# Stick-breaking heads with queries on the partitions: a running sum on VectorE in place of triangular products, and shorter reciprocal roots

## The chip, the cores and the metric

The kernel runs on one core of one Trainium2 chip. The metric is the device time of one execution in microseconds, as the median of three runs. TensorE (PE in the profile) multiplies matrices into PSUM, VectorE (DVE) does elementwise work, ScalarE (ACT) activation functions and casts, SyncE (SP) issues the DMAs.

## The reference

Two layers, each of four additions to a residual of 512 tokens by 1024 channels: a gated feed-forward network, a mixer, a cross attention to 256 memory rows, a second feed-forward network. The change lies in the mixer, which runs 8 stick-breaking heads of width 64 and 4 gated delta-rule heads of width 128 beside each other:

```python
z = einsum('bhtd,bhsd->bhts', qb, kb) * scale
causal = s_idx < t_idx
log_beta = log_sigmoid(z)
log_1m_beta = where(causal, log_beta - z, 0.0)
between = cumsum(log_1m_beta, axis=3, reverse=True) - log_1m_beta
a = where(causal, exp(log_beta + between), 0.0)
out = einsum('bhts,bhsd->bhtd', a, vb)
```

So the weight of key s for query t is exp(z minus the sum of softplus(z) over all keys from s to t). The delta-rule heads (GDN below) normalise q and k, solve a triangular system within a chunk of 128 tokens, and carry a state over four chunks; the outputs of both kinds are normalised by reciprocal roots and go into one output projection.

## The kernel before

Activations are held transposed, channels on the partitions, 512 tokens along the free axis. Every dense weight is split into a rounded part and a rest (`unit`: ScalarE casts, `split_low` L169 subtracts on VectorE), and each dense product is three TensorE products of 512 columns (`mm3`). All TensorE products go through `mm` (L118), transposes through `transpose` (L496).

The order of TensorE's instructions is written out by the program itself: `weave` runs four generators (the norm, `mixer_gdn`, `mixer_sb`, `mixer_dense`) on a planned clock `clk`, which `mm` advances by a planned cost. A generator that yields a number of nanoseconds is taken up again when the clock has passed it, one that yields names waits for `mark`s; the first ready one in that order emits its instructions, so dense projections fill what the chains leave. The numbers set the order alone; on the chip each instruction waits for semaphores. VectorE, ScalarE and the DMA queue are ordered by the framework's scheduler.

`sb_pair` (L583) handles two heads of 64. Scores lie with keys on the partitions: `scores` puts key blocks into three PSUM banks (`SBB`: widths 256, 384+128, 512 queries), each block being a mask product and two products with a split operand. ScalarE makes softplus by Abs (L621), Exp (L622) and Ln (L623), VectorE adds the positive part (L624) and the result is split again. `sums` (L635) then subtracts the running sum over keys on TensorE: each block gets products of `ntri` or `nones` with both parts of every later block, 20 products a head. `weights` takes Exp (L642) and splits; `values` (L649) multiplies by V with `mm3`, 12 products a head, V standing in `vpad` between zeros so that both heads add into one bank.

`gdn_head` (L728) is the chain of one GDN head: norms, a blockwise triangular solve (L809 to L850), four chunk steps (L864 to L886). Its small roots, and those of `sb_pair`, come from `rsqrt`, whose `newton` (L218) is 11 small VectorE operations, each needing the one before.

`mixer_dense` (L948) emits the projections of heads 0 to 3 in turn; from head 2 on it waits for `q0`, `q1` (a GDN head's last chunk) and `qk0`, `qk1` (a pair's last scores). The output projection (`project_out`, L449) takes the pairs' results as `sb0` to `sb3` come, and only its first two output blocks run ahead of `sb3`.

Of the kernel before, what the change touches and what calls it, by code (L numbers as in the profile page):

```python
# [52 lines left out]
class Trunk:  # L53
# [67 lines left out]
    def setup(self):  # L121
# [23 lines left out]
        self.cr = self.sb([P, 2, P], "cr", F32R)  # L145
        self.cb = self.sb([P, 3, P], "cb", BF16)
        self.ntri, self.nones = (self.cr[:, i, :] for i in range(2))
        self.nsb, self.ngd, self.idb = (self.cb[:, i, :] for i in range(3))
        nc.gpsimd.tensor_copy(self.ntri, stage[:, 0:P])
        nc.gpsimd.tensor_scalar(out=self.nones, in0=self.ones, scalar1=-1.0, scalar2=None, op0=ALU.mult)  # L150
# [347 lines left out]
    def gates(self, layer):  # L498
# [36 lines left out]
        yield 12800.0  # L535
# [45 lines left out]
    SBB = (((2, 0, 256),), ((1, 0, 384), (3, 384, 128)), ((0, 0, 512),))  # L581

    def sb_pair(self, layer, pair):  # L583
        nc = self.nc
        mm = self.mm
        t1s = ("s15", "s16", "s17")
        names = [f"s{i}" for i in range(19, 27)]
# [4 lines left out]
        hi, lo = (t.rearrange("p t (j d) -> p t j d", j=3)[:, :, 0:3:2, :] for t in self.vpad)  # L592
        self.split_act(hi, src)
        self.split_low(lo, src, hi)
        self.mark(f"vt{pair}")
        kk, qq, ql = self.qk[pair]
        zs, sp, aa = {}, {}, {}
        av = None

        def split(t, w):  # L600
# [5 lines left out]
            self.split_act(hi, t)  # L606
            self.split_low(lo, t, hi)
            return hi, lo

        def scores(j, n):  # L610
            bl = self.SBB[n]
            z = zs[j, n] = self.bank("at", self.AT)
            w = sum(b[2] for b in bl)
            for i, (s, c, width) in enumerate(bl):
                mm(z[:, c:c + P], self.idb, self.nsb, start=i == 0, stop=False, skip_group_check=True)
                ks = slice(s * P, (s + 1) * P)
                mm(z[:, c:c + width], kk[j][:, ks], qq[j][:, s * P:], start=False, stop=False, skip_group_check=True)
                mm(z[:, c:c + width], kk[j][:, ks], ql[j][:, s * P:], start=False, stop=True, skip_group_check=True)
                yield 200.0
            t1 = self.slot(self.turn("t1", t1s))[:, :w]  # L620
            nc.scalar.activation(t1, z[:, :w], AF.Abs)  # L621
            nc.scalar.activation(t1, t1, AF.Exp, scale=-1.0)  # L622
            nc.scalar.activation(t1, t1, AF.Ln, bias=1.0)  # L623
            nc.vector.scalar_tensor_tensor(out=t1, in0=z[:, :w], scalar=0.0, in1=t1,  # L624
                                           op0=ALU.max, op1=ALU.add)
            hi, lo = split(t1, w)
            for s, c, width in bl:
                sp[j, s] = (hi[:, c:c + width], lo[:, c:c + width])

        def sums(j, n):  # L630
            bl, z = self.SBB[n], zs[j, n]
            for s, c, width in bl:
                for s2 in range(s, NT):
                    for part in sp[j, s2]:
                        mm(z[:, c + (s2 - s) * P:c + width], self.ntri if s2 == s else self.nones, part,  # L635
                           start=False, stop=True, skip_group_check=True)
                    yield 0

        def weights(j, n):
            w = sum(b[2] for b in self.SBB[n])  # L640
            a = self.slot(self.turn("t1", t1s))[:, :w]
            nc.scalar.activation(a, zs[j, n][:, :w], AF.Exp)  # L642
            aa[j, n] = split(a, w)

        def values(j, n):
            hi, lo = aa[j, n]
            for i, (s, c, width) in enumerate(self.SBB[n]):
                vs = slice(64 * j, 64 * j + P)
                self.mm3(av[:, s * P:], (self.vpad[0][:, s, vs], self.vpad[1][:, s, vs]),  # L649
                         (hi[:, c:c + width], lo[:, c:c + width]),  # L650
                         j == 0 and n == 0 and i == 0, True, skip=True)
                yield 0
# [4 lines left out]
        av = self.bank("av", self.AV)  # L657
        for j in range(2):
            yield 1700.0
            for n in range(3):  # L660
                yield from sums(j, n)
                if n < 2:
                    weights(j, n)
                    yield 0
            if j == 0:
                yield from scores(1, 0)
                yield 800.0
            yield from values(j, 0)
            weights(j, 2)
            if j == 0:  # L670
                yield from scores(1, 1)
            yield 0
            yield from values(j, 1)
            yield 0
            if j == 0:
                yield from scores(1, 2)
                self.mark(f"qk{pair}")
                yield 2600.0
# [589 lines left out]
```

## Time and profile before

| | before |
|---|---|
| median of 3 runs | 2524.07 us (2523.88 to 2525.02) |
| profiled execution, its own time | 2528.47 us |
| its span, first to last instruction | 2526.7 us |
| PE busy | 2469.2 us, 98% |
| PE weight loads (beside PE) | 2070.6 us, 82% |
| DVE busy | 1438.3 us, 57% |
| ACT busy | 970.7 us, 38% |
| instructions | 30844 |

Busy time is the time in which at least one instruction of the engine is under way. A TensorE product is listed from its start until its result is out, and the next one starts long before that; what a product costs is read from the distance of two starts. A wait on TensorE that is listed as idle time begins only when the last product has drained.

### The profile page before, as it was taken

To read this page: it belongs to the slowest core of one execution; us is meant where nothing else is said; L and a number is where in the kernel's file an instruction comes from. 1 tells how busy PE (TensorE), PEld (TensorE's weight loads), DVE (VectorE), ACT (ScalarE), POOL (GpSimd) and SP (SyncE) were. 2 spreads that over 40 slices of the span, in tenths; PEclk is the share of its full clock that TensorE was granted. 3 is DMA by queue.
4 is the path that set the end of the run, shared out by engine and by line. 5 is a ranking of instruction groups with operands and counts; after the bars stand their busy time and mean duration, and the time that the engine had idled before them with its cause. 6 is when DMAs were issued, how large, how long until landed. Compare 5 with 4: busy or idle time off the path is not lost.

```text
span 2526.7 us, 30844 instructions
## 1 busy us (share of the span) xinstructions
PE 2469.2 (98%) x12268; PEld 2070.6 (82%) x12268; DVE 1438.3 (57%) x2585; ACT 970.7 (38%) x1545; POOL 10.5 (0%) x21
## 2 busy tenths in 40 slices
PE   8999999999999999999999999999999999999997
PEld 6888887888889888888888888778888988888886
DVE  6443467788675563444554443687876755544345
ACT  4222236555544432222322222466555444322222
POOL 0000000000000000000000000000000000000000
PEclk9999999999999999999999999999999999999999
DMA  5223232111233123332323222311111432322322
GB/s 192 84 100 100 98 94 67 42 51 36 66 110 125 59 92 100 100 101 88 101 95 98 97 89 94 98 59 42 51 43 51 150 101 67 100 85 99 100 94 65
DMA packets 64672, 220.16 MB, mean 87 GB/s; under 512 B 7312, under 2 KB 9616, under 8 KB 64528
## 3 DMA queue, kind: packets, MB, share of 16 engines
q1 hardware_dynamic: 64096, 217.15, 26.5%
q8 instruction: 96, 1.57, 0.3%
q10 hardware_dynamic: 432, 1.04, 0.1%
q14 instruction: 48, 0.39, 0.0%
HBM read 216.07 MB, written 2.10 MB: 86 GB/s over the span
## 4 chain that ended last, share of the span: by engine, by line
PE 89%; DVE 8%; ACT 1%; issue 1%; DMA 0%; DVEq 0%; SPq 0%; ACTq 0%
PE b L118 88%; DVE wlo L169 2%; PE b L496 1%; DVE s L169 1%; ACT whi L164 1%; DVE qkv L713 1%; DVE s L624 0%; DVE s L810 0%; DVE qk L169 0%; DMA wraw<-f1i 0%; DVE s L822 0%; ACT s L164 0%; DVE s L835 0%; DVE s L836 0%; DVE s L429 0%
## 5 line engine op out<-in xcount | busy, mean ns | idle before, releaser
L118 PE MATMUL b<-xh,whi 128*128 128x512 f32 x2112 | 843.6, 399 | 10.1 <-ACT whi L164 8.4
L118 PE MATMUL b<-xh,wlo 128*128 128x512 f32 x2112 | 826.3, 391 | 0.0
L118 PE MATMUL b<-xl,whi 128*128 128x512 f32 x2112 | 825.7, 391 | 0.2
L164 ACT CAST whi<-wraw 128x1024 fp32r<-128x1024 f32 (+1 forms) x408 | 407.9, 1033 | 1033.5 <-PE b L118 947.6
L118 PE MATMUL b<-s,whi 128*128 128x512 f32 (+1 forms) x2136 | 591.6, 364 | 0.2 <-ACT whi L164 0.2
L169 DVE TENSOR_TENSOR wlo<-wraw,whi 128x1024 fp32r<-128x1024 f32 (+1 forms) x408 | 479.3, 1200 | 72.2 <-ACT whi L164 72.0
L118 PEld LDWEIGHTS b<-xh,whi 128*128 128x128 f32 x2112 | 398.7, 189 | 88.7 <-ACT whi L164 8.4
L118 PEld LDWEIGHTS b<-xh,wlo 128*128 128x128 f32 x2112 | 397.6, 188 | 84.8 <-DVE wlo L169 0.8
L118 PEld LDWEIGHTS b<-xl,whi 128*128 128x128 f32 x2112 | 398.6, 189 | 79.2 <-DVE xl L169 1.5
L118 PEld LDWEIGHTS b<-s,whi 128*128 128x128 f32 x2136 | 382.3, 188 | 64.5 <-issue 0.6
L118 PE MATMUL b<-s,wlo 128*128 128x512 f32 (+1 forms) x1068 | 387.1, 362 | 0.0
L352 DVE TENSOR_TENSOR s<-b,rb 128x512 f32<-128x512 f32 x88 | 60.7, 691 | 450.6 <-PE b L118 450.5
L118 PEld LDWEIGHTS b<-s,wlo 128*128 128x128 f32 x1068 | 201.2, 188 | 32.3
L364 DVE TENSOR_TENSOR s<-b,rb 128x512 f32<-128x512 f32 (+1 forms) x98 | 66.3, 680 | 224.8 <-PE b L118 224.7
L164 ACT CAST s<-s 128x512 fp32r<-128x512 f32 x186 | 107.4, 579 | 158.9 <-DVE s L355 124.6
L169 DVE TENSOR_TENSOR s<-s,s 128x512 fp32r<-128x512 f32 x186 | 118.3, 637 | 65.6 <-ACT s L164 65.2
L118 PEld LDWEIGHTS b<-s,s 128*128 128x128 f32 x656 | 84.6, 191 | 13.1 <-issue 8.1
L118 PE MATMUL b<-s,s 128*128 128x128 f32 (+2 forms) x656 | 86.7, 274 | 3.5 <-DVE rqt L224 1.8
L365 DVE SCALAR_TENSOR_TENSOR h<-s,h 128x512 f32<-128x512 f32 (+1 forms) x98 | 63.0, 673 | 0.0
L353 ACT ACTIVATE s<-s 128x512 f32<-128x512 f32 x88 | 54.9, 625 | 17.6 <-DVE s L352 17.6
L118 PE MATMUL b<-s,cr 128*128 128x128 f32 (+3 forms) x320 | 55.1, 311 | 6.6 <-DVE s L169 6.6
L355 DVE TENSOR_TENSOR s<-b,s 128x512 f32<-128x512 f32 x88 | 60.1, 684 | 1.6 <-ACT s L353 1.4
(240 smaller groups left out, 1820.3 us busy)
## 6 DMA issues: line engine op xcount, KB each, us to landing
wraw<-f1i SPq DMA_DIRECT2D x88, 512.0 KB, 3.7
wraw<-f2i SPq DMA_DIRECT2D x88, 512.0 KB, 3.7
wraw<-wi SPq DMA_DIRECT2D x56, 512.0 KB, 3.5
wraw<-f1o SPq DMA_DIRECT2D x32, 512.0 KB, 3.8
wraw<-xkv SPq DMA_DIRECT2D x32, 512.0 KB, 3.5
wraw<-f2o SPq DMA_DIRECT2D x32, 512.0 KB, 4.2
wraw<-wo SPq DMA_DIRECT2D x16, 512.0 KB, 3.5
wraw<-xq SPq DMA_DIRECT2D x16, 512.0 KB, 3.5
```

Source lines behind the costliest of these rows:

```text
L118: self.nc.tensor.matmul(out, lhsT, rhs, **kw)
L164: self.nc.scalar.copy(hi, src)
L169: self.nc.vector.tensor_tensor(lo, src, hi.bitcast(F32), op=ALU.subtract)
L352: nc.vector.tensor_tensor(gt, ps[0], self.rb, op=ALU.mult)
L353: nc.scalar.activation(gt, gt, AF.Silu)
L355: nc.vector.tensor_tensor(m, ps[1], gt, op=ALU.mult)
L364: nc.vector.tensor_tensor(t, p, self.rb[:, cols], op=ALU.mult)
L365: nc.vector.scalar_tensor_tensor(out=h, in0=t, scalar=0.5, in1=h, op0=ALU.mult, op1=ALU.add)
L496: self.nc.tensor.transpose(out, src, self.ident[:src.shape[0], :src.shape[0]])
L713: nc.vector.scalar_tensor_tensor(out=y, in0=cv[:, 1 + i:1 + i + S], scalar=w[i], in1=y, op0=ALU.mult, op1=ALU.add)
```

## The change

Four things change, all in the mixer.

1. `sb_pair` lays the scores out with queries on the partitions (`SBQ`: query blocks of width 512, 384+128, 256 keys). The running sum over keys then lies along the free axis and is one `tensor_tensor_scan` per block on VectorE, backwards; a subtraction and one Exp give the weights. TensorE turns them by ten 128x128 transposes a head (`turned`), three PSUM banks take them by keys, and the split follows from there. `ntri`, `nones` and `sums` are gone.
2. `values` multiplies with V's two parts side by side (`vv`: 64 columns rounded part, 64 columns rest) as one stationary operand, twice for each key block, and the two halves of the bank are added afterwards (one ScalarE copy, one VectorE addition of 64 partitions a head).
3. Four kinds of root, three of each GDN head (`rk`, `rq`, `ro`) and one of each pair (`sn`), go from `newton` to `rsqrt_log`: Ln and Exp on ScalarE and one Newton step of three VectorE operations.
4. The planned waits change, among others `gates` 12800 to 7200, `gdp` 9900 to 11100, the solve's 900/1200/600 to 500/1200/0, the chunk steps' last 200 to 1000, and in `sb_pair` 200, 1700, 800 and 2600 to 600, 11000, 2500 and 500.

```diff
+    def rsqrt_log(self, x, n, tag):
+        nc = self.nc
+        y, t = (self.sb([P, n], tag + c, bufs=2) for c in "yt")
+        nc.scalar.activation(y, x, AF.Ln)
+        nc.scalar.activation(y, y, AF.Exp, scale=-0.5)
+        nc.vector.tensor_tensor(t, y, y, op=ALU.mult)
+        nc.vector.scalar_tensor_tensor(out=t, in0=t, scalar=-0.5, in1=x, op0=ALU.mult, op1=ALU.mult)
+        nc.vector.scalar_tensor_tensor(out=y, in0=t, scalar=1.5, in1=y, op0=ALU.add, op1=ALU.mult)
+        return y
...
+    SBQ = (((3, 0, 512),), ((2, 0, 384), (0, 384, 128)), ((1, 0, 256),))
+    SBK = ((0, 0), (1, 0), (2, 0), (1, 384))
...
+        def scores(j, n):
...
+                mm(z[:, c:c + width], qq[j][:, ts], kk[j][:, :width], start=False, stop=False, skip_group_check=True)
+                mm(z[:, c:c + width], ql[j][:, ts], kk[j][:, :width], start=False, stop=True, skip_group_check=True)
+                yield 600.0
...
+            nc.vector.scalar_tensor_tensor(out=t1, in0=z[:, :w], scalar=0.0, in1=t1,
+                                           op0=ALU.max, op1=ALU.add)
+            run = self.slot(self.turn("run", ("s19", "s20", "s21")))
+            for t, c, width in bl:
+                back = slice(c + width - 1, c - 1 if c else None, -1)
+                nc.vector.tensor_tensor_scan(out=run[:, back], data0=self.ones[:, 0:1].to_broadcast([P, width]),
+                                             data1=t1[:, back], initial=0.0, op0=ALU.mult, op1=ALU.add)
+            nc.vector.tensor_tensor(t1, z[:, :w], run[:, :w], op=ALU.subtract)
+            nc.scalar.activation(t1, t1, AF.Exp)
...
-        def sums(j, n):
-            bl, z = self.SBB[n], zs[j, n]
-            for s, c, width in bl:
-                for s2 in range(s, NT):
-                    for part in sp[j, s2]:
-                        mm(z[:, c + (s2 - s) * P:c + width], self.ntri if s2 == s else self.nones, part,
-                           start=False, stop=True, skip_group_check=True)
...
+            for i in range(2):
+                mm(av[:, s * P:], v, aa[n][i][:, cs], start=s + i == 0, stop=True, skip_group_check=True)
...
+            yield 11000.0
+            at = [self.bank("at", self.AT) for _ in range(3)]
+            for n in range(3):
+                turned(n, at)
+            for n in range(3):
+                weights(n, at)
+            yield 2500.0
```

The program's order shows where this lands. First TensorE, pair 2 of the first layer, head 0: the three score banks are full and dense products (`whi`, `wlo` are a weight's two parts, `xh` the activation) stand ahead. Before, the sums follow (`cr` holds `ntri` and `nones`, `s_...` the split softplus):

```order
L118 MATMUL b_848_4407<-xh_462_2588,wlo_4137 128x512
L118 MATMUL b_858_4449<-s_860_4461,cr_95 128x256 x2
L118 MATMUL b_858_4449<-s_863_4482,cr_95 128x128
L118 MATMUL b_861_4464<-s_863_4482,cr_95 128x384
L118 MATMUL b_861_4464<-s_860_4461,cr_95 128x256 x2
```

In the changed kernel the ten transposes stand in their place (L503 is `transpose`, `cst` the unit matrix), with dense products behind them:

```order
L503 MATMUL b_871_4505<-cst_91,s_848_4356 128x128
L503 MATMUL b_872_4506<-cst_91,s_848_4356 128x128
L503 MATMUL b_871_4505<-cst_91,s_855_4390 128x128
L503 MATMUL b_871_4505<-cst_91,s_859_4413 128x128
L118 MATMUL b_883_4543<-xh_447_2557,whi_4272 128x512
```

The twenty products of a head became ten narrow ones, which read what VectorE and ScalarE have finished of all three banks.

Second, TensorE at the end of the first mixer, the chunk steps of the last GDN head (`yv`, `st`, `rhs` are its small tiles). Before, output projection products stand between them:

```order
L118 MATMUL b_1092_5577<-rhs_5569,s_1050_5383 128x128
L118 MATMUL b_1080_5533<-xh_454_2572,whi_5107 128x512
L118 MATMUL b_1080_5533<-xl_455_2573,whi_5107 128x512
L118 MATMUL b_1080_5533<-xh_454_2572,wlo_5108 128x512
...
L118 MATMUL b_1094_5587<-yv_5579,s_984_5051 128x128
```

In the changed kernel the solve, the chunk steps and the second head's transposes and values (`vv`) of the last pair follow each other, up to the first product that reads the last pair's result:

```order
L118 MATMUL b_1035_5227<-s_1025_5186,vv_4997 128x128
L118 MATMUL b_1053_5318<-s_1047_5282,s_992_5023 128x128 x4
L118 MATMUL b_1055_5327<-s_998_5044,s_1046_5281 128x128 x4
...
L118 MATMUL b_1077_5399<-rhs_5373,s_1046_5281 128x128
L118 MATMUL b_1079_5403<-yv_5401,s_978_4952 128x128
L118 MATMUL b_1082_5411<-s_1072_5388,vv_4997 128x512
...
L503 MATMUL b_1107_5488<-cst_91,s_1106_5486 128x128 x4
L118 MATMUL b_1033_5219<-xh_1108_5494,whi_4957 128x512
```

No dense product is left between these rows: there are 41 small products outside the transposes, 14 transposes and 8 value products from the second row to the last but one.

Third, VectorE over the same stretch of the changed kernel (L625 adds the positive part, L630 is the scan, L632 the subtraction, L844 to L853 belong to the solve):

```order
L625 SCALAR_TENSOR_TENSOR s_1040_5250<-b_1036_5228,s_1040_5250 128x512
L630 SCALAR_TENSOR_TENSOR s_1041_5255<-cst_91,s_1040_5250 128x512
L844 TENSOR_TENSOR s_998_5044<-b_1053_5318,cst_91 128x512
L632 TENSOR_TENSOR s_1040_5250<-b_1036_5228,s_1041_5255 128x512
L625 SCALAR_TENSOR_TENSOR s_1048_5289<-b_1044_5271,s_1048_5289 128x512
L849 TENSOR_TENSOR s_1047_5282<-s_1047_5282,b_1055_5327 128x512
L630 SCALAR_TENSOR_TENSOR s_1049_5294<-cst_91,s_1048_5289 128x384
```

VectorE now holds the head's running sums and the solve's updates in one queue, in turn.

## Rows read from the trace of the kernel before

**Rows 1.** The page: busy time by engine, and the chain that ended last.

```profile
PE 2469.2 (98%) x12268; PEld 2070.6 (82%) x12268; DVE 1438.3 (57%) x2585; ACT 970.7 (38%) x1545; POOL 10.5 (0%) x21
...
PE 89%; DVE 8%; ACT 1%; issue 1%; DMA 0%; DVEq 0%; SPq 0%; ACTq 0%
```

**Rows 2.** Windows, the two mixers: length, busy us (instructions) by engine, granted clock, DMA.

```profile
380.00:736.00 356.00, 338.92 (x1929) 286.97 (x1927) 273.02 (x683) 198.78 (x379) 0.52 (x1) 0.99 0.17 55
1630.00:1985.00 355.00, 338.31 (x1932) 286.08 (x1931) 272.56 (x682) 199.64 (x380) 0.00 (x0) 1.00 0.18 56
```

**Rows 3.** Waits of TensorE, first mixer: idle us in total, times, longest.

```profile
PE b L118 <- DVE s L771: 4.9, 3, 1.7
PE b L118 <- DVE s L169: 4.4, 9, 0.8
...
PE b L118 <- ACT s L164: 0.8, 4, 0.2
```

**Rows 4.** The page, costliest groups: the products of `sums`, whole program.

```profile
L118 PE MATMUL b<-s,cr 128*128 128x128 f32 (+3 forms) x320 | 55.1, 311 | 6.6 <-DVE s L169 6.6
```

**Rows 5.** Timeline of TensorE, values of one pair: start, us, instruction, [idle before].

```profile
597.03 0.65 PE L118 MATMUL b<-s,cr 128*128 128x256 f32 x4
597.52 0.45 PE L118 MATMUL b<-s,vph 128*128 128x256 f32 x2
...
599.29 0.33 PE L118 MATMUL b<-s,vpl 128*128 128x384 f32 x1
599.46 1.05 PE L118 MATMUL b<-s,s 128*128 128x128 f32 x8
600.26 0.42 PE L118 MATMUL b<-s,vph 128*128 128x128 f32 x2
600.52 0.27 PE L118 MATMUL b<-s,vpl 128*128 128x128 f32 x1
600.63 0.67 PE L118 MATMUL b<-s,vph 128*128 128x512 f32 x2
601.14 0.40 PE L118 MATMUL b<-s,vpl 128*128 128x512 f32 x1
601.38 0.39 PE L118 MATMUL b<-xh,whi 128*128 128x512 f32 x1
```

**Rows 6.** Timeline of TensorE, four transposes of 128x128 and what follows.

```profile
473.19 0.60 PE L496 MATMUL b<-cst,s 128*128 128x128 f32 x4
473.62 0.39 PE L118 MATMUL b<-rhs,s 128*128 128x128 f32 x2
```

**Rows 7.** Timeline of VectorE: one root of a GDN head, first and last operations.

```profile
553.50 0.16 DVE L761 TENSOR_SCALAR ss<-ss 128x4 f32<-128x4 f32 x1
...
559.36 0.16 DVE L225 TENSOR_TENSOR rkt<-rkt,rkm 128x4 f32<-128x4 f32 x1
559.56 0.16 DVE L226 SCALAR_TENSOR_TENSOR rky<-rkt,rky 128x4 f32<-128x4 f32 x1
```

**Rows 8.** Groups by form, VectorE, first mixer: busy us, mean ns of one, idle before.

```profile
L169 DVE TENSOR_TENSOR wlo<-wraw,whi 128x1024 fp32r<-128x1024 f32 x34 | 41.2, 1220 | 1.0 <-ACT whi L164 1.0
...
L624 DVE SCALAR_TENSOR_TENSOR s<-b,s 128x512 f32<-128x512 f32 x16 | 10.9, 679 | 2.0 <-ACT s L623 2.0
...
L624 DVE SCALAR_TENSOR_TENSOR s<-b,s 128x256 f32<-128x256 f32 x8 | 3.2, 405 | 0.0
```

**Rows 9.** The same view for ScalarE.

```profile
L623 ACT ACTIVATE s<-s 128x512 f32<-128x512 f32 x16 | 10.1, 631 | 0.3
```

**Rows 10.** Timeline of TensorE, end of the first mixer.

```profile
693.13 0.49 PE L118 MATMUL b<-yv,s 128*128 128x128 f32 x2 [0.38 <-DVE yv L870]
...
701.96 1.31 PE L496 MATMUL b<-cst,s 128*128 128x128 f32 x8 [0.41 <-DVE s L989]
```

**Rows 11.** Windows around an idle stretch of TensorE; the column behind POOL is the granted clock.

```profile
408.00:411.00 3.00, 1.12 (x8) 1.09 (x8) 1.25 (x3) 2.97 (x3) 0.00 (x0) 0.88 0.11 42
411.00:414.00 3.00, 3.00 (x12) 2.67 (x12) 0.23 (x1) 2.90 (x12) 0.00 (x0) 0.55 0.00 0
```

More of the change, by code (lines that the diff above doesn't have):

```diff
@@ L586, in sb_pair @@
         t1s = ("s15", "s16", "s17")
-        names = [f"s{i}" for i in range(19, 27)]
+        names = [f"s{i}" for i in range(22, 27)]
         yield (f"sbp{pair}",)
@@ L600, in split @@
-        def split(t, w):
+        raw, aa = {}, {}
+        def scores(j, n):
+            bl = self.SBQ[n]
+            z = self.bank("at", self.AT)
+            w = sum(b[2] for b in bl)
+            for i, (t, c, width) in enumerate(bl):
+                mm(z[:, c + width - P:c + width], self.nsb, self.idb, start=i == 0, stop=False, skip_group_check=True)
+                ts = slice(t * P, (t + 1) * P)
+                mm(z[:, c:c + width], qq[j][:, ts], kk[j][:, :width], start=False, stop=False, skip_group_check=True)
+                mm(z[:, c:c + width], ql[j][:, ts], kk[j][:, :width], start=False, stop=True, skip_group_check=True)
+                yield 600.0
+            t1 = raw[n] = self.slot(self.turn("t1", t1s))[:, :w]
+            nc.scalar.activation(t1, z[:, :w], AF.Abs)
+            nc.scalar.activation(t1, t1, AF.Exp, scale=-1.0)
+            nc.scalar.activation(t1, t1, AF.Ln, bias=1.0)
+            nc.vector.scalar_tensor_tensor(out=t1, in0=z[:, :w], scalar=0.0, in1=t1,
[7 more added lines that the diff above has]
+            nc.scalar.activation(t1, t1, AF.Exp)
@@ L601, in split, with turned, weights @@
+        def turned(n, at):
+            for t, c, width in self.SBQ[n]:
+                for s in range(t + 1):
+                    i, c2 = self.SBK[s]
+                    c2 += (t - s) * P
+                    self.transpose(at[i][:, c2:c2 + P], raw[n][:, c + s * P:c + (s + 1) * P])
+        def weights(n, at):
+            w = sum(b[2] for b in self.SBQ[n])
             if w <= S // 2:
@@ L605, in split @@
                 hi, lo = (self.slot(self.turn("sbs", names), F32R)[:, :w] for _ in range(2))
[L606 to L626, printed above, removed]
-            for s, c, width in bl:
-                sp[j, s] = (hi[:, c:c + width], lo[:, c:c + width])
@@ L645, in values @@
[L645 to L652, printed above, removed]
+            self.split_act(hi, at[n][:, :w])
+            self.split_low(lo, at[n][:, :w], hi)
@@ L656, in sb_pair @@
             yield 0
-        av = self.bank("av", self.AV)
+        o = self.slot(("s0", "s1", "s13", "s37")[pair])
         for j in range(2):
-            yield 1700.0
+            yield 11000.0
+            at = [self.bank("at", self.AT) for _ in range(3)]
             for n in range(3):
[L661 to L678, printed above, removed]
-            yield from values(j, 2)
-        o = self.slot(("s0", "s1", "s13", "s37")[pair])
-        nc.scalar.copy(o, av)
+                turned(n, at)
+            for n in range(3):
+                weights(n, at)
+            yield 2500.0
+            av = self.bank("av", self.AV)
+            for s in range(NT):
+                if j == 0 and s < 3:
+                    yield from scores(1, s)
+                    if s == 2:
+                        self.mark(f"qk{pair}")
+                values(j, s, av)
+                yield 500.0 if s < 3 else 0
+            own, other = slice(64 * j, 64 * j + 64), slice(64 - 64 * j, P - 64 * j)
+            low = self.slot(self.turn("t1", t1s))
+            nc.scalar.copy(low[own], av[other])
+            nc.vector.tensor_tensor(o[own], av[own], low[own], op=ALU.add)
         sq = self.slot(self.turn("t1", t1s))
@@ L717, in gdn_project @@
         self.qkv[head] = [qkv[:, j, :] for j in range(3)]
-        self.mark(f"gdp{head}", 9900.0)
+        self.mark(f"gdp{head}", 11100.0)
     def after(self, i):
@@ L814, in gdn_head @@
                     tt(v3(qt)[:, 2 * i:2 * i + 2, :], half(i)[:, :, 0, :], v3(dm)[:, 2 * i:2 * i + 2, :], op=ALU.mult)
-            yield 2000.0 if n else 3400.0
+            yield 2200.0 if n else 4200.0
             b = gd()
@@ L837, in gdn_head @@
         for n in range(len(small), len(LEVELS)):
-            yield 900.0 if n > len(small) else 2200.0
+            yield 500.0 if n > len(small) else 3300.0
             b = gd()
@@ L865, in gdn_head @@
                     op0=ALU.mult, op1=ALU.add)
-            yield 900.0 if c else 1600.0
+            yield 900.0 if c else 1500.0
             b = gd()
```

48 lines of the change are left out of this document (18 added, 30 removed).

## The prediction, made before the changed kernel ran

> **What bounds the kernel now.** I read the page first, then the windows of the two mixers, then TensorE's waits in them, then single stretches. TensorE is busy 98% of the span and 89% of the chain that ended last is its own work [rows 1], so a product taken away from it is time gained, as long as something else is ready to run. The mixers are the two stages with slack: TensorE stands idle 356.0 - 338.9 = 17.1 us in the first and 16.7 us in the second, while VectorE is busy 273 of 356 us, 77% [rows 2]. Most of that idle time is in a few places: three waits of 1.6 us for L771, which follows a root of the GDN head, and thirteen short ones (4.4 + 0.8 us) for the splits that feed `sums` and `values` [rows 3]. All of the change is inside the mixers, so I sum it for one mixer and double it.
>
> **TensorE's work.** Distances of starts give the price of a product by width [rows 5]: 512 columns 601.38 - 601.14 = 0.24 us, 384 columns 599.46 - 599.29 = 0.17, 256 columns (597.52 - 597.03) / 4 = 0.12, 128 columns 600.63 - 600.52 = 0.11. The row of eight full-precision entries takes 0.80 us, two entries to a product, so 0.20 a product.
> - `sums` goes. Per head it has, for both parts, one product of 512, two of 384, three of 256 and four of 128 columns: 2 x (0.24 + 0.34 + 0.36 + 0.44) = 2.76 us. Sixteen heads: 44.2 us. The page lists 55.1 us for these 320 products [rows 4], with waits under way in it; I take 44.2 and count the waits apart.
> - The third product of `values` goes: 0.24 + 0.17 + 0.12 + 0.11 = 0.64 us a head, 10.2 us.
> - Ten transposes a head come: (473.62 - 473.19) / 4 = 0.108 us each [rows 6], 1.08 us a head, 17.3 us.
> - The scores keep the same number of products and columns. Sum: -44.2 - 10.2 + 17.3 = -37.1 us, or **-18.6 us per mixer**.
>
> **Work on other engines.** No DMA is added or moved: SP issues the same weight loads, in step with the products that use them. POOL loses two small constants at the start, behind which no one waits. Per head ScalarE loses three casts and gains one copy; each of 16 roots a mixer gives it two small operations. VectorE loses eight of eleven root operations of 0.16 us (16 x 8 x 0.16 = 20.5 us per mixer) and gains the scan and one 64-partition addition a head. The trace has no scan. Below, its price is bounded by one elementwise pass over 512 elements, 0.68 us; above by the pass over twice as many, 1.22 us [rows 8]. In a scan each element needs the one before, and where VectorE's operations need each other their starts lie 0.20 us apart (559.36 to 559.56) [rows 7], longer than the 0.16 each lasts, so I take the upper end: 2.5 x 1.22 = 3.05 us for a head's 1280 columns. VectorE then has 273 - 20.5 + 8 x (3.05 + 0.68) = 282 us per mixer and stays under TensorE.
>
> The Trainium skill (DVE: opcode table, instruction layouts, handler registers and perf-mode slots, section 6, on feedback) says that the built-in scan runs at half throughput, which speaks against moving sums to VectorE. With the elementwise price instead, the chain at the mixer's end would be 2.5 x 0.54 = 1.4 us shorter, and the sum 2.7 us lower.
>
> **Waits that go.** The waits for L771 are the end of a root: from 553.50 to 559.72 eleven dependent operations, with large ones let in between [rows 7]. Two on ScalarE and three on VectorE replace them, half as many hand-overs, so some 3 us earlier against a wait of 1.6: these go, though the planned wait there falls from 3.4 to 2.6 us. The thirteen waits of `sums` and `values` go with their places. A wait costs its idle time and the drain before it: a 512 product lasts 0.40 us but the next starts 0.24 after it [rows 5], so 0.16 more. 4.9 + 5.2 + 16 x 0.16 = **-12.7 us per mixer**.
>
> **Waits that come in the middle.** The transposes of a head wait for the last Exp of three banks. ScalarE needs 3 x 0.63 us for the first bank [rows 9], VectorE then 2.5 x 0.68 for the positive parts, 2.5 x 0.68 for the subtractions and 3.05 for the scans, 8.3 us in all if VectorE did nothing else; at the load above its other work stretches that past the planned 11 us and the 2.4 us of yields in the scores. If it holds there is no wait; if VectorE interleaves as much as it does before, it is late by about what the old waits took. Ends: 0 and 12.7 us. I take 0.8 us for seven heads, **+5.5 us**.
>
> **The end of the mixer.** This is the place that can spoil the gain. TensorE has 18.6 us less work while the pair's chain has become longer, so dense work runs out before the last pair is done. In the program's order the last stretch holds 41 full-precision products, 14 transposes and 8 value products and no dense one: 41 x 0.20 + 14 x 0.108 + 2 x 0.64 = 11.0 us of work. The chain through it, for the second head: VectorE's queue of positive parts, subtractions and scans with five updates of the solve between (1.7 + 1.7 + 3.05 + 3.4 = 9.9 us), the last Exp (0.4), transposes and drain (1.3), a cast and three subtractions (0.6 + 1.7), the last values and drain (0.5), copy, addition, square (0.6 + 0.7 + 0.6), column sums and drain (1.0), a root of six small steps (1.2), widening (0.4), transposes and drain (0.6), scaling and cast (0.7 + 0.6): 20.8 us, by 0.68 and 0.63 for a full tile, 0.40 for a half and 0.20 for a small step [rows 7 to 9]. Idle: 20.8 - 11.0 = 9.8 us. Today two waits of 0.38 and 0.41 us stand there [rows 10]. Net **+9.0 us per mixer**; ends +5 (solve and head not in turn) and +14.
>
> **The clock.** After 1.88 us without a product the granted clock is 0.88 and then 0.55 for a window [rows 11], so some of that end will run at the lower level, 1.2 GHz. Its 11.0 us of products would take twice as long, most of it inside waits. Ends 0 and 11; I take **+3 us per mixer**.
>
> **Sum.** -18.6 - 12.7 + 5.5 + 9.0 + 3 = -13.8 us per mixer, -27.6 in all. The profiled execution took 2528.47 us with a span of 2526.7; it becomes 2500.9. The median of three is 4.4 us below it, so **2496.5 us** against 2524.07. Own range of this case: 2484 to 2508.
>
> **Rivals.**
> - *The end stays covered* (10%). If the planned waits overstate the chains, GDN steps and pair end together as today; then neither the 9.0 nor the 3 us come: -25.8 us per mixer, 2472 us. For it: the present end has hardly a wait [rows 10]. Against: the order leaves no dense product there.
> - *The waits only move* (18%). ScalarE's two steps queue behind casts, and the transposes are late by all that the splits were: 12.7 in place of 5.5, so 14.4 us more, 2511 us. For it: VectorE's 77% load [rows 2].
> - *The clock falls for the whole end* (10%). All 11.0 us double on the path, and the output projection starts at 1.2 GHz as the products at 411 to 414 do [rows 11], 1.5 us: 12.5 in place of 3, 19 us more, 2515 us. The Trainium skill (TensorE: Matmul & The Clock Gate, Part 1) says that the slower clock is the array's default and activity releases it. That agrees with rows 11, and it gives this rival its chance.
> - *The scan becomes the bound: slower* (7%). At t us for 512 elements each head's chain grows by 2.5 x (t - 1.22), in eight places a mixer. The gain of 13.8 us is eaten at t = 1.22 + 13.8 / 20 = 1.9 us, nearly three elementwise passes [rows 8]. At 2.44, twice the upper bound, it is 24.4 - 13.8 = +10.6 us per mixer, 2545 us. For it: reading backwards, and no scan in the trace. Against: a bound that covers two passes already.
> - That the change does not do what it says is no case of its own: the program's order shows the sums gone.
>
> **Numbers.** The forecast has 55%. A run of this kernel can tell about 0.2%, 5 us, from no change. Faster by more: the forecast whole (55), the covered end (10), most of the moved waits (16) and of the clock (6), 87%. Within 5 us: the rest of these two and the edge of the scan case, 7%. Slower: 6%. The range from 2478 to 2517 leaves out most of the covered end, the scan, and the worst of the clock, under 2 in 10.
>
> **What would show it.** In the changed profile: no products of `cr`, 160 more transposes, TensorE's instruction count lower by some 220 and its mixers busy some 19 us less; waits for L774 (the old L771) gone; the scan's rows at about 1.2 us for 512 elements and 0.9 for 384; in the last 20 to 25 us before the output projection TensorE half idle, with a granted clock under 1; VectorE at 80% or more of the mixers. The forecast is wrong if that end shows under 3 us of idle time, if waits before L503 sum to over 8 us a mixer, or if scans take over 1.9 us.

## The result, and the profile after

The changed kernel took 2500.77 us (median of 4 runs, 2497.03 to 2501.99) against 2523.98 for the kernel before beside it: ratio 0.9905, 95% interval 0.9888 to 0.9922. The forecast was 2496.5 in a range of 2478 to 2517. The profiled execution took 2501.99 us with a span of 2500.2; before it was 2528.47 and 2526.7, so the profiles lie 26.5 us apart. Outside the mixers they differ by 0.3 us. From the first product of the gates to the first of the cross attention, they last 346.0 and 340.4 us in place of 357.2 and 355.3: -11.2 and -15.0, where -13.8 each was forecast.

The page, the lines that answer to [rows 1]:

```profile
PE 2443.2 (98%) x12044; PEld 2037.1 (81%) x12044; DVE 1449.4 (58%) x2405; ACT 957.9 (38%) x1567; POOL 9.0 (0%) x19
...
PE 88%; DVE 9%; ACT 1%; issue 1%; DMA 0%; DVEq 0%; ACTq 0%
```

TensorE has 224 instructions less, as counted in advance, but its busy time falls by 26.0 us and not by the 37.1 counted. Most of the difference is that more of what is left runs at a lower clock.

The windows, with the columns of [rows 2]: the two mixers, then three stretches of the first.

```profile
380.00:725.00 345.00, 328.46 (x1818) 272.52 (x1816) 279.28 (x594) 192.72 (x390) 0.52 (x1) 0.97 0.17 57
1618.00:1958.00 340.00, 324.08 (x1821) 268.75 (x1820) 278.75 (x594) 192.85 (x390) 0.00 (x0) 0.98 0.17 58
542.00:549.00 7.00, 7.00 (x26) 6.14 (x25) 3.67 (x22) 3.42 (x18) 0.00 (x0) 0.52 0.01 2
658.00:668.00 10.00, 7.57 (x35) 6.34 (x34) 6.63 (x15) 4.65 (x11) 0.00 (x0) 0.67 0.00 1
675.00:685.00 10.00, 6.58 (x17) 4.79 (x17) 3.97 (x15) 1.45 (x5) 0.52 (x1) 0.50 0.01 2
```

TensorE stands idle 345.0 - 328.5 = 16.5 us in the first mixer and 15.9 in the second, almost what [rows 2] gave before (17.1 and 16.7), though the old waits are gone. VectorE stands at 81%. The granted clock of 0.52, 0.67 and 0.50 marks three stretches at the lower of its two levels, 1.2 GHz, for most or all of the time.

TensorE's waits in the first mixer, as in [rows 3]:

```profile
PE b L118 <- DVE s L844: 3.6, 5, 1.2
PE b L118 <- DVE yv L873: 2.3, 6, 0.5
PE b L503 <- DVE rot L220: 1.9, 1, 1.9
PE b L118 <- DVE s L813: 1.5, 4, 0.5
PE b L118 <- ACT xh L160: 1.5, 1, 1.5
...
PE b L503 <- DVE s L700: 0.9, 1, 0.9
```

No wait for the root (L774, before L771) and none for the splits of `sums` is left. L844 and L813 belong to the solve, L873 to the chunk steps. The transposes L503 never wait for the heads' weights. Two of their waits, 1.9 and 0.9 us, are for the normalisation of a pair (for the first the profile names L220, but what those transposes read is the widened root of L695, which ends just after it). The third, 0.4 us for a gate (L989), stood there before too [rows 10]. For the account of the prediction, the other waits of TensorE in the kernel before, 380 to 690 us, beside those of [rows 3]; they sum to 5.9 us:

```profile
PE b L496 <- ACT qkv L715: 1.9, 1, 1.9
PE b L118 <- DVE st L878: 1.8, 4, 0.4
PE b L118 <- DVE rqt L224: 0.9, 3, 0.3
...
PE b L118 <- DVE s L835: 0.7, 4, 0.2
PE b L118 <- DVE s L262: 0.6, 1, 0.6
```

Groups by form, VectorE, first mixer, as in [rows 8]:

```profile
L625 DVE SCALAR_TENSOR_TENSOR s<-b,s 128x512 f32<-128x512 f32 x16 | 10.9, 683 | 1.2 <-ACT s L624 1.2
...
L630 DVE TENSOR_TENSOR_SCAN s<-cst,s 128x512 f32<-128x512 f32 x8 | 9.8, 1220 | 0.1
L630 DVE TENSOR_TENSOR_SCAN s<-cst,s 128x384 f32<-128x384 f32 x8 | 7.6, 948 | 0.0
```

The scan takes 1220 ns for 512 elements, the value taken in advance (1.22), and 948 for 384.

Timeline of TensorE, first in the middle of the first mixer, then at its end:

```profile
541.51 0.70 PE L503 MATMUL b<-cst,qkv 128*128 128x128 f32 x4
542.02 2.08 PE L118 MATMUL b<-cst,g 128*128 128x128 f32 x8
...
545.46 0.77 PE L118 MATMUL b<-xh,whi 128*128 128x512 f32 x1
546.03 0.63 PE L118 MATMUL b<-xl,whi 128*128 128x512 f32 x1
546.46 0.63 PE L118 MATMUL b<-xh,wlo 128*128 128x512 f32 x1
...
676.91 1.09 PE L503 MATMUL b<-cst,s 128*128 128x128 f32 x4 [1.90 <-DVE rot L220]
679.52 0.79 PE L118 MATMUL b<-xh,whi 128*128 128x512 f32 x1 [1.52 <-ACT xh L160]
...
685.11 0.46 PE L118 MATMUL b<-xh,whi 128*128 128x512 f32 x1
```

At the lower level a 512 product starts 0.43 us after the one before it (546.46 - 546.03), in place of 0.24 [rows 5]. At the end the output projection begins so: from 679.52 to 685.11 its first 12 products take 5.6 us, where 12 x 0.24 would be 2.9. The end before had waits of 0.38 and 0.41 us [rows 10]; waits of that kind are still there, and 1.90 and 1.52 us have come in front of the output projection.

### The profile page after: what moved, and what is told of

Same layout as the page of the kernel before. It is cut to its first block, busy times and chain, and to the rows that moved or that the text cites. A ratio compares the mean times of both kernels' runs of the same rounds, so it can differ in the third digit from the quotient of the medians.

```text
span 2500.2 us, 30165 instructions
## 1 busy us (share of the span) xinstructions
PE 2443.2 (98%) x12044; PEld 2037.1 (81%) x12044; DVE 1449.4 (58%) x2405; ACT 957.9 (38%) x1567; POOL 9.0 (0%) x19
## 4 chain that ended last, share of the span: by engine, by line
PE 88%; DVE 9%; ACT 1%; issue 1%; DMA 0%; DVEq 0%; ACTq 0%
PE b L118 87%; PE b L503 1%; DVE qkv L716 1%; DVE s L630 1%; DVE wlo L165 1%; DVE s L625 1%; DVE s L632 0%; DVE s L844 0%; ACT whi L160 0%; DMA wraw<-f1i 0%; DVE s L813 0%; DVE s L853 0%; DVE s L849 0%; DVE s L825 0%; DVE s L838 0%
## 5 line engine op out<-in xcount | busy, mean ns | idle before, releaser
L165 DVE TENSOR_TENSOR wlo<-wraw,whi 128x1024 fp32r<-128x1024 f32 (+1 forms) x408 | 479.0, 1200 | 70.9 <-ACT whi L160 70.6
L160 ACT CAST s<-s 128x512 fp32r<-128x512 f32 x90 | 55.2, 614 | 125.2 <-DVE s L362 124.6
L118 PE MATMUL b<-s,s 128*128 128x128 f32 (+2 forms) x656 | 86.1, 275 | 12.9 <-DVE s L844 7.2
L165 DVE TENSOR_TENSOR s<-s,s 128x512 fp32r<-128x512 f32 x90 | 61.2, 682 | 56.7 <-ACT s L160 56.4
L165 DVE TENSOR_TENSOR s<-b,s 128x512 fp32r<-128x512 f32 (+1 forms) x92 | 56.6, 635 | 29.8 <-ACT s L160 29.8
L160 ACT CAST s<-b 128x512 fp32r<-128x512 f32 (+1 forms) x92 | 46.5, 553 | 44.4 <-PE b L118 22.7
```

The costliest lines, as they stand in the source:

```text
L118: self.nc.tensor.matmul(out, lhsT, rhs, **kw)
L160: self.nc.scalar.copy(hi, src)
L165: self.nc.vector.tensor_tensor(lo, src, hi.bitcast(F32), op=ALU.subtract)
```

## The experiments

Times are medians; each ratio is to runs of the kernel before on the same chip. All edits are to the changed kernel unless said otherwise.

**The price of the sums.** In scan_twice:

```diff
-            for t, c, width in bl:
+            for t, c, width in (*bl, *bl):
                 back = slice(c + width - 1, c - 1 if c else None, -1)
```

> The changed kernel with every running sum computed twice in place, so each head costs VectorE 2.5 x 1.22 = 3.05 us more and the output stays. Theory A (the sums lie under cover in the middle and on the path only at a mixer's end, one head or two there): 3 to 6 us per mixer, 2507 to 2513. Theory B (VectorE at 81% is close to its limit, every head is on the path): 8 x 3.05 = 24.4 us per mixer, 2550. Theory C (the sums are nowhere on the path): within 2 us of 2501.

And in no_scan:

```diff
-                nc.vector.tensor_tensor_scan(...)
-            nc.vector.tensor_tensor(t1, z[:, :w], run[:, :w], op=ALU.subtract)
+            nc.vector.tensor_tensor(t1, z[:, :w], t1, op=ALU.subtract)
```

> The changed kernel without the running sum: the subtraction takes the unsummed softplus, so this leaves out the sum over keys. Each head's chain is 3.05 us shorter. Theory A (on the path only at the end of a mixer): 3 to 6 us per mixer less, 2489 to 2495. Theory B (VectorE as the bound): up to 24 us per mixer less, 2452 to 2475. Theory C (the end is set by the solve and the chunk steps of the last GDN head, not by the sums): within 2 us of 2501.

Doubled: 2545.48 us, 1.0079 (1.0064 to 1.0094), that is 44.7 us more, of 16 x 3.05 = 48.8 us of added scans. The time is close to theory B, but not because VectorE is full: it is busy 303 of 364 us in the first mixer there, 83%, hardly more than the 81% without the addition. Left out: 2500.20, 0.9900 (0.9883 to 0.9916), theory C. So the kernel stands at a bend: a head's chain that is 3 us shorter gives nothing, one that is 3 us longer counts almost in full. The waits of scan_twice show the second half (TensorE, first mixer):

```profile
PE b L503 <- DVE s L632: 6.0, 6, 2.2
PE b L118 <- DVE s L165: 4.0, 2, 2.0
```

Now the transposes do wait for the heads, six times, 1.0 us each on average, so they had some 2 us in hand before (3.05 less 1.0, an estimate); the values then wait for their splits. TensorE's other products stand behind such a wait too: in the timeline of gdn_waits_old below nothing starts from 491.24 to 496.82. By the table at the end of this section TensorE's idle time grows by 28.2 of the 42.2 us between the two profiles; some 6 us are the lower clock, and 8 us have no cause shown.

**The planned wait that goes with it.** scan_twice_14 and no_scan_8 change one line more each, to the length that the chain then has:

```diff
-            yield 11000.0
+            yield 14000.0
```

> The changed kernel with every running sum computed twice, as in scan_twice (2545.5), and with the planned wait ahead of the transposes 14000 in place of 11000. Theory A (in scan_twice TensorE stood behind late transposes because the order did not allow for them; VectorE itself has room): at least half of the 44 us go, 2501 to 2523. Theory B (VectorE is the bound at that load): 2535 to 2550.

> The changed kernel without the running sum (the sum over keys is left out), as in no_scan, and with the planned wait ahead of the transposes 8000 in place of 11000, so that the order uses the 3.05 us that each head's chain is shorter. no_scan with the planned wait kept took 2500.2. Theory A (the order fixes the chain, so the sum costs time through its planned wait: eight heads of 3 us, partly covered): 4 to 8 us per mixer less than no_scan, 2484 to 2492. Theory B (the solve and the chunk steps of the GDN heads set the length of the mixer): within 3 us of 2500.

No theory held: both runs came out above every range. scan_twice_14 took 2593.18, 1.0268 (1.0254 to 1.0282): 47.7 us more than scan_twice. In its profile TensorE's idle time is 32.9 us longer, and the lower clock costs about 14.5 us more. no_scan_8, which has 8000 there, took 2525.23, 0.9998 (0.9989 to 1.0007): 25 us more than no_scan, with a chain that is both shorter and planned shorter. The first long stop shows one reason. TensorE, then VectorE:

```profile
434.47 1.26 PE L503 MATMUL b<-cst,s 128*128 128x128 f32 x10
...
441.66 0.23 PE L118 MATMUL b<-cb 128*128 128x128 bf16 x1 [2.46 <-DVE s L165]
```

```profile
440.25 0.74 DVE L715 SCALAR_TENSOR_TENSOR qkv<-cv,gn,qkv 128x512 f32<-128x512 f32 x1
440.92 1.61 DVE L165 TENSOR_TENSOR s<-b,s 128x512 fp32r<-128x512 f32 x3
```

The transposes are ready in time at 434.47, but the splits behind them now meet the convolution (L715) and the solve in VectorE's queue and run at 440.92; TensorE stands 2.46 us. Such waits for the splits (L165) sum to 8.1 us in each mixer, where no_scan has none. In all TensorE is idle 12.0 us longer than in no_scan, and the lower clock costs about 13.7 us more, most of it in the second mixer. The planned wait does not only say when a pair is ready, it also says which of the GDN head's steps it meets on VectorE.

**The price of TensorE's products.** third_product puts a third product into `values`; third_same_order does the same without telling the planned clock:

```diff
-            for i in range(2):
-                mm(av[:, s * P:], v, aa[n][i][:, cs], start=s + i == 0, ...)
+            for m, i in enumerate((0, 0, 1)):
+                mm(av[:, s * P:], v, aa[n][i][:, cs], start=s + m == 0, ...)
```

```diff
-                mm(av[:, s * P:], ...)
+                (nc.tensor.matmul if m == 1 else mm)(av[:, s * P:], ...)
```

> The changed kernel with three products for each key block in values, as before the change (the rounded weights are multiplied twice, so the output is not the reference's). Theory A, the term of the prediction: TensorE's own work sets the time, so 16 heads x 0.64 = 10.2 us come back: 2500.8 + 10.2 = 2511. Theory B, the chains set it: TensorE stands idle 16.5 us in each mixer waiting for chains, so products added in the middle come out of later idle time and the time moves by under 4 us (2501 to 2505).

> As third_product (a third product for each key block in values, 0.64 us a head, 10.2 us in all), but the planned clock does not count it, so TensorE keeps the order of the changed kernel with the added products next to their twins. third_product, in its own order, took 2522.6, 21.8 more than the changed kernel. Theory A (the price of a product is its own time, the rest of the 21.8 came from the other order): 2508 to 2512. Theory B (the chains set the length of a mixer and idle time absorbs the products): 2501 to 2506. Theory C (order is not the cause): 2518 to 2526.

In its own order the added product cost 21.8 us, twice its price: 2522.55, 0.9990 (0.9981 to 0.9999), above the ranges of both theories. In the order of the changed kernel it cost 4.6 us, half its price: 2505.33, 0.9915 (0.9901 to 0.9930). The number is that of theory B, but its reason does not hold. The two mixers of third_same_order, in the columns of [rows 2], and the stretches of them at the lower clock:

```profile
380.00:726.00 346.00, 329.99 (x1848) 274.34 (x1847) 279.62 (x594) 191.97 (x390) 0.52 (x1) 0.98 0.18 57
1619.00:1963.00 344.00, 327.99 (x1855) 272.05 (x1853) 280.23 (x595) 193.19 (x391) 0.00 (x0) 0.99 0.18 57
...
662.20:669.00 6.80, 6.03 (x24) 5.19 (x25) 2.57 (x7) 2.70 (x7) 0.00 (x0) 0.50 0.00 0
675.90:686.10 10.20, 6.78 (x19) 5.01 (x19) 3.96 (x15) 1.77 (x7) 0.52 (x1) 0.50 0.01 2
1914.90:1921.70 6.80, 4.70 (x12) 3.34 (x13) 3.03 (x8) 0.74 (x2) 0.00 (x0) 0.50 0.00 0
```

Idle time took up nothing to speak of: it is 346.0 - 330.0 = 16.0 us in each mixer, after 16.5 and 15.9. What differs is the clock: 12.9 + 4.7 us of TensorE's busy time lie at the lower level, against 19.7 + 8.4 in the changed kernel (table below). At half speed that gives back 5.2 us, and 10.2 - 0.5 - 5.2 = 4.5, and the two mixers are 4.6 longer. So theory A's price holds. Whether the added products kept the clock up or this is the scatter of the last section, no run here separates: the changed kernel's four executions had a mean clock of 0.991, 0.991, 0.991 and 0.993, these four 0.993 and 0.994.

In its own order idle time grows by 4.2 and 4.5 us in the two mixers. Two waits account for it (the first mixer):

```profile
PE b L503 <- DVE s L700: 3.1, 1, 3.1
PE b L118 <- ACT s L686: 2.5, 1, 2.5
```

The first (0.9 in the changed kernel) lies in the middle, at 557 us: a pair's scaling stands on VectorE behind the first steps of a solve. The second, new, lies at the end, at 682 us: the last pair's square now follows the last GDN head with nothing beside it.

**The roots, and the waits of the GDN heads.** newton_back undoes the roots alone in the changed kernel (`rsqrt_log` back to `rsqrt` at rk, rq, ro, sn); roots_only makes them alone in the kernel before; gdn_only adds the nine new planned waits of the gates and GDN heads to that; gdn_waits_old is the changed kernel without these nine. The edit of the last:

```diff
-        yield 7200.0
+        yield 12800.0
...
-        self.mark(f"gdp{head}", 11100.0)
+        self.mark(f"gdp{head}", 9900.0)
...
-            yield 1000.0
+            yield 200.0
```

> The changed kernel with its four kinds of root computed again by eleven VectorE operations, the new planned waits kept. Theory A (the root sits on the GDN chain; its late end stopped TensorE three times a mixer for 1.6 us, and the last pair's root lies on the end of a mixer): 3 x 1.8 + 6 x 0.2 = 6.6 us per mixer, 2514. Theory B (20.5 us more of VectorE work per mixer lengthen every chain that dense work no longer covers): 10 to 20 us per mixer, 2521 to 2541. Theory C (the new planned waits alone removed those stops): within 4 us of 2501.

> The kernel before with the four shorter roots alone, all planned waits as they were. gdn_only, which also takes the new planned waits of the GDN heads, took 2556.6. Theory A (the roots by themselves remove the three waits for L771 with their drains, and the order still fits): 2510 to 2516. Theory B (TensorE's order waits 3.4 us there in any case, so the earlier root is not used): within 5 us of 2524.

> The kernel before with the four shorter roots and the new planned waits of the gates and the GDN heads, but with its old scores, sums and values. Theory A (the terms add up: here only the waits for the old L771 go, 3 x 1.6 plus their drains, and the root at the end): 2524 less 11 to 14, 2510 to 2513. Theory B (the roots pay only together with the new sums, because it is VectorE's load that they relieve): within 5 us of 2524. Theory C (planned waits set for other chains do harm here): over 2529.

> The changed kernel with the planned waits of the gates and the GDN heads as before the change, its new scores, sums, values, roots and the waits in sb_pair kept. With the roots alone the kernel before took 2514.8 (0.9954 of before), the whole change 0.9905. Theory A (what the new scores and values save comes without the new GDN waits): within 5 us of the changed kernel, 0.9885 to 0.9925. Theory B (the order carries it: with the old waits the GDN heads and the pairs end apart and the saved products come out of idle time): 0.995 to 1.01. Theory C (the new GDN waits cost time, as in gdn_only): under 0.9885.

| | scores and values | roots | GDN waits | us | ratio |
|---|---|---|---|---|---|
| roots_only | old | new | old | 2514.83 | 0.9954 (0.9937 to 0.9970) |
| gdn_only | old | new | new | 2556.60 | 1.0116 (1.0100 to 1.0131) |
| gdn_waits_old | new | new | old | 2553.12 | 1.0110 (1.0093 to 1.0127) |
| newton_back | new | old | new | 2530.76 | 1.0023 (1.0013 to 1.0032) |
| changed kernel | new | new | new | 2500.77 | 0.9905 (0.9888 to 0.9922) |

The roots alone give 0.0046 of 2524, 11.6 us: theory A. The two mixers of roots_only:

```profile
380.00:728.00 348.00, 336.04 (x1928) 284.27 (x1927) 259.19 (x555) 202.36 (x411) 0.52 (x1) 1.00 0.18 57
1622.00:1970.00 348.00, 336.61 (x1931) 284.62 (x1929) 258.52 (x553) 202.90 (x411) 0.00 (x0) 1.00 0.18 57
```

TensorE stands idle 12.0 and 11.4 us, about 5 us less in each mixer than in [rows 2]: the three waits of 1.6. Their drains are not seen by themselves.

The new scores with the old waits are slower than the kernel before (just above theory B), and so are the old scores with the new waits (theory C); old with old and new with new are the fast ones. In gdn_waits_old TensorE stops twice for 5 us in the first mixer. The first of them, TensorE and then VectorE:

```profile
491.24 0.60 PE L503 MATMUL b<-cst,s 128*128 128x128 f32 x4
496.82 1.11 PE L503 MATMUL b<-cst,s 128*128 128x128 f32 x4 [4.98 <-DVE s L700]
...
499.23 0.63 PE L118 MATMUL b<-xl,whi 128*128 128x512 f32 x1
```

```profile
486.98 0.43 DVE L695 COPY s<-sny 128x512 f32<-128x512 f32 x1
...
492.30 0.90 DVE L807 COPY s<-s 32x128 f32<-32x128 f32 x4
...
495.36 0.74 DVE L716 SCALAR_TENSOR_TENSOR qkv<-cv,gn,qkv 128x512 f32<-128x512 f32 x1
496.02 0.74 DVE L700 SCALAR_TENSOR_TENSOR s<-s,gn,b 128x512 f32<-128x512 f32 x1
```

The pair's last scaling (L700) meets the next GDN head at the start of its solve and stands behind it on VectorE; the next pair's first transposes need its bank and stop TensorE, and the products after the stop are 0.43 us apart. In the changed kernel that scaling starts at 484.46, ahead of the solve. newton_back, with a time in theory B's range, has a root that is longer than planned: of the 11.7 us that TensorE stands idle longer in its first mixer, 3.0 are waits for L774, 2.5 for the root itself (L232, L233) and 3.9 for splits (L165).

**The end of the mixer.** gates_early turns and scales GDN heads 0 to 2 before the end and puts their 18 products ahead of the last pair's; hold_two moves 12 products that are there already:

```diff
+        def first():
+            yield from gated(range(3), self.GD, ("s12",))
+            yield from turned(0)
+        early = [first(), turned(1), turned(2), *(self.until() for _ in range(3)), turned(3)]
...
+                                    (0, 1, 2, 4, 5, 6, 3, 7))
```

> The changed kernel with another order of the output projection: the gated results of GDN heads 0 to 2 are turned and split as soon as the last head's solve runs (their transposes go to the GDN banks), and the first two output blocks take them ahead of the last pair's result, so 18 products of 512 columns (4.1 us) are left for the stretch in which the mixer's end has no dense work. Theory A (the end is idle for want of dense work): 4 us of idle time are filled in each mixer and less of the stretch runs at the lower clock, 8 to 14 us in all, 2487 to 2493. Theory B (the end is bound by VectorE, and the three gates, 3 x 1.36 us, now queue ahead of the solve): what is filled is given back, within 4 us of 2501. Theory C: VectorE is so full there that it becomes slower, 2505 to 2510.

```diff
+        self.mark(f"n{pair}")
...
+        self.mark(f"w{pair}")
...
+            if p == 2:
+                yield ("w3",)
+                return
             yield (f"sb{p}",)
             ops.append(self.to_x(p, self.sbo[p]))
+            if p == 1:
+                yield ("sb2",)
+                ops.append(self.to_x(2, self.sbo[2]))
+                yield ("n3",)
```

> The changed kernel with 12 products of the output projection held back: those of pairs 1 and 2 for the first two output blocks go behind the column sums of the last pair (6) and behind its last transposes (6), into the two waits of 1.9 and 1.5 us. No work is added or taken away. Theory A (the clock falls because TensorE has almost nothing to do there, and the output projection starts at the lower level): the first 13 products of the projection go from 0.43 to 0.23 us apart, 2.6 us per mixer, 2494 to 2497. Theory B (what is held back is missing from the solve's stretch ahead of it, which goes idle or slow by as much): within 3 us of 2501. Theory C (the stretch ahead drops to the lower clock for longer): slower, 2505 to 2510.

gates_early took 2520.46, 0.9976 (0.9968 to 0.9985), worse than its theory C. Its three sets of transposes follow each other on two banks and one buffer, and the third waits for the scaling (L990 there) of an earlier one:

```profile
642.06 0.60 PE L503 MATMUL b<-cst,s 128*128 128x128 f32 x4
647.58 1.11 PE L503 MATMUL b<-cst,s 128*128 128x128 f32 x4 [4.92 <-DVE s L990]
```

So it does not tell whether more dense work at the end would pay; it made a new stop ahead of it. hold_two took 2496.75 (2496.26 to 2497.29), 0.9881 (0.9866 to 0.9896), the lowest time of all and within theory A's figures. Its first mixer ends so:

```profile
670.24 0.77 PE L118 MATMUL b<-xh,whi 128*128 128x512 f32 x1
...
672.95 0.83 PE L503 MATMUL b<-cst,s 128*128 128x128 f32 x4
...
675.28 0.49 PE L118 MATMUL b<-xh,whi 128*128 128x512 f32 x1
676.00 0.50 PE L118 MATMUL b<-xl,whi 128*128 128x512 f32 x1 [0.23 <-DVE xl L165]
```

The two waits are filled, 6 products run at the lower level in place of 12, and behind one short wait the projection goes on at 0.23 to 0.34 us a product. But idle time is no shorter over the mixer (16.4 us, with other waits in it): the gain is the clock alone. Its interval overlaps that of the changed kernel, its second mixer is 1.7 us longer (342.1 against 340.4; the solve, now without dense products, runs at the lower level there), and some of the first mixer's gain, about 3.4 us, is the stretch at 542 to 549, which stayed at the full clock in this run (the last section has its row). That it is the better kernel is likely, not shown.

**Where the time went, run by run.** For the two mixers of each profile: length, TensorE's idle time, and TensorE's busy time within stretches whose granted clock is the lower level. A product takes about twice as long there (0.43 us for 0.24), so about half of the last pair of columns is lost.

| | length, us | idle | busy at the lower level |
|---|---|---|---|
| before | 357.2, 355.3 | 17.1, 16.7 | 6.8, 3.4 |
| roots_only | 349.3, 348.8 | 12.0, 11.6 | 0, 0 |
| changed kernel | 346.0, 340.4 | 16.5, 16.1 | 19.7, 8.4 |
| third_same_order | 347.3, 343.7 | 16.0, 16.1 | 12.9, 4.7 |
| third_product | 354.8, 352.2 | 20.7, 20.6 | 18.6, 13.1 |
| no_scan | 345.1, 339.3 | 15.8, 15.8 | 19.8, 7.0 |
| no_scan_8 | 351.6, 356.3 | 22.1, 21.5 | 21.2, 32.9 |
| scan_twice | 364.2, 364.5 | 30.6, 30.2 | 19.1, 20.8 |
| scan_twice_14 | 388.2, 388.1 | 47.0, 46.7 | 34.3, 34.5 |
| newton_back | 357.1, 356.5 | 28.2, 27.8 | 16.4, 16.1 |
| gdn_only | 372.8, 369.9 | 21.3, 20.2 | 27.2, 24.4 |
| gdn_waits_old | 368.8, 369.4 | 34.5, 34.6 | 25.4, 28.0 |
| gates_early | 353.5, 353.1 | 24.7, 24.3 | 18.7, 18.8 |
| hold_two | 339.3, 342.1 | 16.4, 15.6 | 3.4, 12.7 |

The kernel before has such stretches too, one of them in [rows 11].

## Why the prediction was right, and where its steps were not

The time came within the range, and each mixer's -11.2 and -15.0 average to -13.1 us where -13.8 was forecast. Part of this is luck: terms that were off by up to 5 us cancelled.

- **TensorE's work, -18.6 us per mixer.** The counts came as said: no `cr` products, 160 more transposes, 224 instructions less. The price holds as well, but it is not the gain. From roots_only to the changed kernel the mixers get 11.7 us shorter (12.4 by the ratios), of the 37.1 counted. Given back are 9.0 us of new idle time and about 14.0 us of clock (28.1 us of busy time at the lower level, none in roots_only); 2.3 us have no cause shown. The sign of some 19 us less busy time in a mixer did not come: it is 10.7 and 14.4.
- **Waits that go, -12.7.** The waits went, 10.1 us of idle time in a mixer. Of the 2.6 us that were counted for drains no run shows anything by itself. The roots' share was 10.8 us by that working; roots_only gave 11.6, with 10.2 us less idle time in its profile.
- **Waits in the middle, +5.5.** This is the step that failed, in size and in place. The waits up to 640 us sum to 6.4, but the kernel before had 5.9 us there besides those counted as going, so only 0.5 was added. And the transposes, which were to be late, are on time; solve, chunk steps and a pair's scaling make these waits.
- **The mixer's end, +9.0.** Forecast were 9.8 us of idle time, and the waits from 640 to 690 us sum to 9.3. But the chain of that working went through VectorE's running sums, and no_scan shows that they are not on it: the end is the last GDN head's solve and chunk steps, and behind them the last pair's normalisation, 1.9 + 1.5 us without any work. TensorE is idle 7.3 of the 25 us up to 680, under a third, where half was forecast.
- **The clock, +3.** Too small by a third: 4.5 us on the average of two unlike mixers. The lower level took half of 19.7 - 6.8 us more in the first, 6.5 us, and half of 8.4 - 3.4 in the second, 2.5. The forecast looked only at the end, and the fall at 542 follows chunk steps without dense products beside them, not a long idle time. Of the rival of the falling clock a part came: the output projection does start at 1.2 GHz.
- **Sum.** First mixer -18.6 - 0.6 (idle time 17.1 to 16.5) + 6.5 = -12.7, measured -11.2; second -18.6 - 0.6 + 2.5 = -16.7, measured -15.0. So 1.5 and 1.7 us stay without a cause. Against the forecast, idle time came 5.0 us lower in a mixer; the clock (1.5 more), the drains (2.6) and the rest without a cause (1.6) took that up.
- **The median.** In the profiles 2501.99 us stand against 2500.9 forecast. The 4.4 us by which the median lay below the profile before were carried over; in the changed kernel it is 1.2.
- **The scan.** Price as taken. The rival in which it becomes the bound gave 2545 us at 2.44 us for 512 elements; scan_twice is that case and took 2545.48. That the two agree so closely is luck: the start was 4.3 us higher than forecast and the addition 4.1 us smaller than 48.8.
- **What had no term.** The new planned waits of the GDN heads were priced at nothing, but for a clause on the root. With the old ones the same code takes 2553.12. The forecast was right because the waits were set so that both chains fit; it had not shown that they do, and its own question, what each VectorE step meets in the queue, was put only to the mixer's end.

## What to carry to other kernels

Where an order is written from planned waits, these are part of the price: a chain shorter than its wait gives nothing, a longer one stops every instruction behind it, and a wait that fits its own chain can still put it behind another on a shared engine. To price work in such a stage, add it once with the order kept and once with the order free, and read the idle time and the granted clock beside both. Here the same products cost 4.6 and 21.8 us, and in both profiles their own work is 10.2: the rest is idle time and clock. A time within a theory's range does not yet show its reason. And look for what can be kept back for the last serial steps of a stage, as it fills their waits and may let more of the next stage run at the full clock (6 products at the lower level in hold_two's first mixer, 12 without it).

## What the runs showed of the hardware

The scan costs (1220 - 948) / 128 = 2.1 ns for an element, an elementwise pass with an addend from PSUM (683 - 404) / 256 = 1.1 (L625 takes 404 ns for 256): twice as much, also when it reads backwards. This agrees with what the Trainium skill says (DVE: opcode table, instruction layouts, handler registers and perf-mode slots, section 6), half throughput.

The granted clock of one stretch of the same program differs from run to run. In the changed kernel 542 to 549 us has 0.52 (above); in hold_two, which is the same program up to there and whose TensorE stands idle just as long in the 7 us before (1.5 us in both), the windows read:

```profile
535.00:542.00 7.00, 5.46 (x34) 4.36 (x33) 5.15 (x11) 3.37 (x9) 0.00 (x0) 1.00 0.25 82
542.00:549.00 7.00, 7.00 (x41) 5.79 (x40) 4.86 (x24) 4.64 (x23) 0.00 (x0) 1.00 0.00 0
```

Busy 7.00 us both times, 41 instructions here and 26 there. In the second mixer of the changed kernel the same steps ran at 1.00 as well. So in this stretch, short products with small waits ahead of dense ones, the clock fell in one execution and not in another, and a difference of 3.4 us between two such profiles (half of 6.8) can be this alone.
